# One layer kernel: rows of a tile reordered to (step of chunk, chunk), and the work between the projections laid at fixed steps

## The chip, the cores and the metric

The kernel runs on one core of a Trainium2 chip. The metric is the device time of one execution in microseconds (us); a kernel's time is the median over its runs. The profile records one more execution, with a start and an end for the instructions of each engine: TensorE (PE, with PEld for its weight loads), VectorE (DVE), ScalarE (ACT), GpSimd (POOL) and the queues that issue transfers (SP, and one at ACT).

## What is computed

One layer over 256 rows of width 2048, in float32:

```python
x = x + 0.5 * swiglu(rms_norm(x, ffn1_norm), w_gate, w_up, w_down)       # FFN 1, width 5632
u, q, k, v = split(rms_norm(x, mix_norm) @ w_in)                         # 1024 columns each
y_ssm = S5(u)       # 64 groups of 16 channels, 64 complex states each; z = gelu(y); z * sigmoid(z @ w_glu + b_glu)
y_sb  = sb(rms_norm(q), rms_norm(k), v)                                  # 8 heads of 128
x = x + concat(rms_norm(y_ssm), rms_norm(y_sb)) @ w_out
x = x + 0.5 * swiglu(rms_norm(x, ffn2_norm), ...)                        # FFN 2
x = x + rms_norm((p @ w_ple_proj) * sigmoid(rms_norm(x) @ w_ple_gate))
```

S5 is a diagonal complex recurrence along the rows. The attention has no softmax. With z the scaled score of a query with a key before it, the weight is `exp(log_sigmoid(z) + the sum of log_sigmoid(-z) over the keys between them)`, and 0 for keys that are not before the query.

## The kernel before

**Products.** Each float32 factor is split into two fp32r parts, hi (a cast on ACT, L169) and lo (a subtraction on DVE, L170); a product is hi*hi + lo*hi + hi*lo (L283, L284, L288). `gemm_block` makes 256 rows by 512 columns. It walks the inner dimension in halves of a quarter: a half is 256 inner rows, 12 matmuls of 512 columns. A quarter of the weights (1024 KB) is one transfer on SP into one of three `raw` tiles; its two halves are split into one of four hi and four lo tiles. After each half `step()` is called.

**Steps.** Everything that stands beside the products is attached to steps. `start(g)` puts a generator on a list, and `step()` moves each of them on by one `yield`; `put_off(n, f)` calls `f` at the (n+1)-th step from then. So instructions are written down between the halves. A planner that orders each engine's stream by its own estimates of time may move an instruction ahead of others that it takes to be later; `pin` ties an instruction behind the one written just before it on its engine. The products themselves are not pinned.

**Stages.** FFN 1 also prepares the S5 coefficients (`s5_prep`) and writes them to scratch in DRAM, for four parts q of 16 groups each. Then the layer's middle runs, which the change touches: the projections u (16 halves), q0, k0, q1, k1 (32 halves), v (16 halves), the GLU product of S5 (8 halves of 24 matmuls with 256 columns), and `w_out` (32 halves, the attention side first for each block of columns). After that come FFN 2 and the last embedding.

**S5.** `u_block` takes 512 columns of u out of PSUM; `u_turn` turns them on PE (L678) and brings them on ACT in 32 copies (L686, both halves of u) into an order of (step of chunk, channel) on the partitions. A chunk is 4 rows, so that there are 64 chunks. For each part q, one generator then goes on by a stage per step: the loads from scratch; state matmuls (L705); products with a rotation on DVE (L714 to L717); two sums and two scans over the chunks (L719 to L723); the products back and the shift by one chunk (L728 to L735), where POOL clears the first column (L733); output matmuls (L745 to L749); 16 gelu activations of 32 partitions (L759). POOL writes the decays `dec` (L697) ahead of that. The state matmuls and the output matmuls are four steps apart.

**q and k.** `qk_block` takes a block out on ACT (L773), squares it on DVE (L774), sums (L776), scales each head (L778); at the fourth step after the block PE turns it (L788) and DVE scales it (L792).

**Attention.** Four pairs of heads go through `scores` (with a large negative mask), `logs` (Abs, Exp, Ln on ACT; two DVE instructions on PSUM, L833 and L834) and `weights` (the sums over keys as matmuls into a second PSUM tile, L844 to L851, a subtraction on DVE, L852, and Exp, L853), one stage of one pair per step, all during v. `attn_out` runs during the GLU product. Tiles `aux` in PSUM, two of them, hold everything here that is not a `gemm_block`. `rms` sums the squares (ACT, then POOL, L884) with a matmul (L868).

## Time and profile before

| | |
|---|---|
| runs, median (lowest to highest) | 1942.05 us (1936.94 to 1943.15) |
| the profiled execution | 1942.49 us, of which the span of the profile is 1940.7 us |
| mean granted PE clock in it | 0.991 |
| busy: PE, DVE, ACT, POOL | 1902.7, 1315.6, 1127.0, 36.1 us |
| the layer's middle (u to `w_out`) | from 747.7 to 1111.1 us |

Times in the profile are counted from the start of the span. In a group's row, "x48 | 58.0, 1223 | 42.6 <-ACT" means 48 instructions, 58.0 us busy, 1223 ns for one, and 42.6 us in which the engine was idle just before them, mostly until ACT released them. In a row of the timeline the first two numbers are the start and the duration; a bracket holds the idle time before it and what ended it. Matmuls overlap, so their pitch is read from their starts. A row of windows gives, for each engine, the busy time and the number of instructions, and then the granted PE clock, the DMA share and GB/s.

### The profile page before, as it was taken

The numbers are of one execution on the slowest core, as the hardware profiler recorded it, in microseconds if no ns is written. First come the engines' busy times: TensorE is split into PE (matmuls) and PEld (weight loads), VectorE is DVE, ScalarE is ACT, GpSimd is POOL, SyncE is SP. The second block draws the span as 40 slices with busy tenths as digits, with TensorE's granted clock in tenths as the row PEclk, the third lists the DMA queues.
The fourth block names the chain that finished last, engine by engine and source line by source line (L and its number), as shares of the span: only waits on it lengthen the run. The fifth ranks groups of instructions, "written<-read, shape, count | busy, mean of one in ns | idle before, by whom it ended". The sixth has DMA issues, their size and how long they took to land.

```text
span 1940.7 us, 24021 instructions
## 1 busy us (share of the span) xinstructions
PE 1902.7 (98%) x9148; PEld 1574.8 (81%) x9148; DVE 1315.6 (68%) x1629; ACT 1127.0 (58%) x1294; POOL 36.1 (2%) x52
## 2 busy tenths in 40 slices
PE   9999999999999999988999999999999999999997
PEld 7887788888888888866897888888888888888886
DVE  8995765555688896576666755555555568998855
ACT  7466564444578885746765554444444457887754
POOL 0000000000000000010011000000000000000000
PEclk9999999999999999989999999999999999999999
DMA  9677777666656667554446566666667566666653
GB/s 322 224 229 252 255 239 235 201 212 202 213 191 198 206 206 258 202 203 163 130 159 198 189 194 201 209 215 198 216 195 213 185 222 202 199 205 204 214 189 126
DMA packets 220964, 401.45 MB, mean 207 GB/s; under 512 B 12080, under 2 KB 41904, under 8 KB 220720
## 3 DMA queue, kind: packets, MB, share of 16 engines
q1 hardware_dynamic: 208368, 385.13, 61.1%
q10 hardware_dynamic: 12480, 14.78, 2.1%
q8 instruction: 71, 1.16, 0.2%
q14 instruction: 45, 0.37, 0.1%
HBM read 369.46 MB, written 14.68 MB: 198 GB/s over the span
## 4 chain that ended last, share of the span: by engine, by line
PE 77%; DVE 6%; ACT 4%; issue 2%; DMA 2%; SPq 1%; POOL 1%; DVEq 0%; ACTq 0%; POOLq 0%
PE acc L284 25%; PE acc L283 25%; PE acc L288 24%; DVE wlo L170 2%; DMA raw<-in_ffn_w_down 1%; DVE hlo L170 1%; ACT whi L169 1%; SPq L215 1%; DVE nlo L179 1%; ACT hhi L169 1%; ACT zt L759 1%; DMA dv<-in_ssm_b_laid 0%; DVE cm L544 0%; DMA ceq<-in_ssm_c_laid 0%; DVE mid L202 0%
## 5 line engine op out<-in xcount | busy, mean ns | idle before, releaser
L170 DVE TENSOR_TENSOR wlo<-raw,whi 128x1024 fp32r<-128x1024 f32 x666 | 810.5, 1225 | 460.5 <-ACT whi L169 446.4
L169 ACT CAST whi<-raw 128x1024 fp32r<-128x1024 f32 x666 | 696.6, 1053 | 704.4 <-PE acc L284 647.6
L283 PE MATMUL acc<-whi,nhi 128*128 128x512 f32 x1568 | 618.3, 394 | 4.4 <-ACT whi L169 4.0
L284 PE MATMUL acc<-whi,nlo 128*128 128x512 f32 x1568 | 613.9, 392 | 0.0
L288 PE MATMUL acc<-wlo,nhi 128*128 128x512 f32 x1568 | 421.9, 390 | 0.8 <-DVE wlo L170 0.8
L284 PE MATMUL acc<-whi,hlo 128*128 128x512 f32 x1056 | 411.9, 390 | 0.7 <-DVE hlo L170 0.2
L283 PE MATMUL acc<-whi,hhi 128*128 128x512 f32 x1056 | 411.2, 389 | 0.0
L283 PEld LDWEIGHTS acc<-whi,nhi 128*128 128x128 f32 x1568 | 295.9, 189 | 68.7 <-ACT whi L169 4.9
L288 PEld LDWEIGHTS acc<-wlo,nhi 128*128 128x128 f32 x1568 | 295.0, 188 | 63.7 <-DVE wlo L170 2.0
L284 PEld LDWEIGHTS acc<-whi,nlo 128*128 128x128 f32 x1568 | 296.4, 189 | 60.2
L288 PE MATMUL acc<-wlo,hhi 128*128 128x512 f32 x1056 | 282.3, 389 | 0.0
L284 PEld LDWEIGHTS acc<-whi,hlo 128*128 128x128 f32 x1056 | 198.3, 188 | 44.5 <-DVE hlo L170 3.3
L288 PEld LDWEIGHTS acc<-wlo,hhi 128*128 128x128 f32 x1056 | 198.3, 188 | 41.2
L283 PEld LDWEIGHTS acc<-whi,hhi 128*128 128x128 f32 x1056 | 198.2, 188 | 40.7
L170 DVE TENSOR_TENSOR hlo<-hT,hhi 128x1024 fp32r<-128x1024 f32 x88 | 188.2, 2139 | 49.1 <-ACT hhi L169 49.1
L169 ACT CAST hhi<-hT 128x1024 fp32r<-128x1024 f32 x88 | 192.2, 2185 | 1.7 <-DMA raw<-in_ffn_w_gate 1.7
L202 DVE STREAM_TRANSPOSE mid<-h 128x512 f32<-128x512 f32 x44 | 47.2, 1159 | 0.0
L426 DVE SCALAR_TENSOR_TENSOR h<-acc,sm,sg 128x512 f32<-128x512 f32 x44 | 31.0, 746 | 19.4 <-PE acc L288 19.4
L759 ACT ACTIVATE zt<-aux 32x128 f32<-32x128 f32 x64 | 25.0, 390 | 28.2 <-PE aux L749 27.5
L748 PE MATMUL aux<-rt,cpr 128*64 128x64 f32 x128 | 17.4, 278 | 11.7 <-issue 7.0
L406 ACT ACTIVATE sg<-acc,sm 128x512 f32<-128x512 f32 x44 | 27.7, 682 | 0.4 <-DVE sm L195 0.3
L748 PEld LDWEIGHTS aux<-rt,cpr 128*64 128x64 f32 x128 | 16.4, 191 | 12.4 <-issue 7.5
(233 smaller groups left out, 840.8 us busy)
## 6 DMA issues: line engine op xcount, KB each, us to landing
raw<-in_ffn_w_up SPq DMA_DIRECT2D x88, 1024.0 KB, 5.5
raw<-in_ffn_w_down SPq DMA_DIRECT2D x88, 1024.0 KB, 5.1
raw<-in_ffn_w_gate SPq DMA_DIRECT2D x86, 1024.0 KB, 5.2
raw<-in_w_in SPq DMA_DIRECT2D x32, 1024.0 KB, 5.4
raw<-in_w_out SPq DMA_DIRECT2D x16, 1024.0 KB, 5.2
raw<-in_w_ple_gate SPq DMA_DIRECT2D x16, 1024.0 KB, 5.1
hT<-mid SPq DMA_DIRECT2D x160, 64.0 KB, 4.9
h<-mid SPq DMA_DIRECT2D x128, 32.0 KB, 4.0
```

What stands on the lines that cost most here:

```text
L169: nc.scalar.copy(hi, src)
L170: nc.vector.tensor_tensor(out=lo, in0=src, in1=hi.bitcast(F32), op=ALU.subtract)
L179: nc.vector.scalar_tensor_tensor(out=lo[:, j, :], in0=src[:, j, :], scalar=scale, in1=hi[:, j, :].bitcast(F32), op0=ALU.mult, op1=ALU.subt ...
L202: nc.vector.transpose(mid[:, :, t, :, k0 : k0 + nk].rearrange("p q b f -> p f q b"), src.rearrange("p (f q b) -> p f q b", f=nk, q=4),)
L215: nc.sync.dma_start(out[32 * q : 32 * q + 32, :, 32 * i : 32 * i + 32, :], mid[32 * i : 32 * i + 32, q])
L283: nc.tensor.matmul(ps[t], lhsT=lh, rhs=hi[:, j, :], start=start and j == 0, stop=False)
L284: nc.tensor.matmul(ps[t], lhsT=ll, rhs=hi[:, j, :], start=False, stop=False)
L288: nc.tensor.matmul(ps[t], lhsT=lh, rhs=lo[:, j, :], start=False, stop=stop and j == 1)
L406: nc.scalar.activation(sg[:, t * NB : (t + 1) * NB], pg[t], AF.Silu, scale=xn.rs(t))
L426: nc.vector.scalar_tensor_tensor(out=hh[:, t * NB : (t + 1) * NB], in0=pu[t], scalar=xn.rs(t), in1=sg[:, t * NB : (t + 1) * NB], op0=ALU.m ...
L748: nc.tensor.matmul(o, lhsT=ld["cpr"][:, cs], rhs=pr[:, rs], start=False, stop=False)
L759: nc.scalar.activation(zv[32 * r : 32 * r + 32, 2 * (q % 2) : 2 * (q % 2) + 2, :, t], yv[32 * t : 32 * t + 32, :, r, :], AF.Gelu_apprx_tanh,)
```

## The change

The host hands x, its turned copy and p to the kernel with the rows of each tile of 128 in the order (step of chunk, chunk), so that partition 32*s + c holds row 4*c + s, and puts the output's rows back. The masks of the attention follow that order: a small input `not_ahead` is loaded through SP in place of two POOL instructions. With this order:

- `u_turn` is two DVE transposes in blocks of 32 by 32. The 16 PE transposes and the 32 ACT copies go.
- S5's stages are put off to fixed steps: part q has its state matmuls at step 12 + 8q, counted from the first half of u, then its DVE stages at +3, +4 and +5, its output matmuls at +7 and gelu at +9. DVE handles real and imaginary parts in one instruction; the first column is cleared on DVE; the decays and the loads for part q have steps of their own, and `rot` has two tiles. Gelu is one activation of 128 partitions, followed by 16 transfers of 32 KB per pair of parts that bring the channels to the partitions.
- q/k: squares and scaling move to ACT, the turn is at the fifth step, and the scaling follows two steps later.
- Attention: each stage of a pair has its own step. The sums over keys are accumulated into the scores' own PSUM tile with masks of -1, so that L834, L852 and the second tile go. Pairs 0 and 1 begin at steps 5 and 6 of v, pairs 2 and 3 at steps 17 and 19, which are steps 1 and 3 of the GLU product. `attn_out` comes at step 16 and at step 28 (the fourth half of `w_out`).
- v is taken out of PSUM on ACT. `w_out` begins with the S5 side of the first two blocks of columns; the sum for S5's norm is one step later.
- Most matmuls of S5 and of the attention are pinned.

```diff
-        for to, op, scale in ((tri_r, ALU.is_gt, 1.0), (late_r, ALU.is_ge, -(2.0 ** 100))):
-            u = com("h")[:, :P]
-            nc.gpsimd.affine_select(
-                out=u, in_=ones, compare_op=op, fill=0.0, base=0, pattern=[[-1, P]], channel_multiplier=1
-            )
-            nc.scalar.activation(to, u, AF.Copy, scale=scale)
+
+        u = com("h")[:, :P]
+        nc.sync.dma_start(u, a["not_ahead"])
+        nc.scalar.activation(tri_r, u, AF.Copy, scale=-1.0)
+        nc.scalar.activation(late_r, u, AF.Copy, scale=-(2.0 ** 100))
         nc.scalar.copy(ident_r, ident)
-        nc.scalar.copy(ones_r, ones)
+        nc.scalar.activation(all_r, ones, AF.Copy, scale=-1.0)
...
-        put_off(2, u_turn, pool, n, us)
+        put_off(1, u_turn, pool, n, us)
 
     def u_turn(pool, n, us):
-        pt = aux()
+        ua[n] = get(pool, f"ua{n}")
         for t in range(TT):
-            for b in range(4):
-                pin(nc.tensor.transpose(
-                    pt[:, b * T + t * P : b * T + (t + 1) * P], us[:, t * NB + b * P : t * NB + (b + 1) * P], ident
-                ))
-        ua[n] = get(pool, f"ua{n}")
-        pv = pt.rearrange("p (b c s) -> p b c s", b=4, s=SL)
-        uv = ua[n].rearrange("p (b q c) -> p b q c", b=4, q=4)
-        for q in range(4):
-            for s in range(SL):
-                nc.scalar.copy(uv[32 * s : 32 * s + 32, :, q, :], pv[32 * q : 32 * q + 32, :, :, s])
+            nc.vector.transpose(
+                ua[n].rearrange("p (r t c) -> p r t c", t=TT, c=32)[:, :, t, :],
+                us[:, t * NB : (t + 1) * NB].rearrange("p (r h) -> p r h", h=32),
+            )
 
     def s5_main(pool, zpool):
...
+        def load(q, names):
+            for n in names:
+                ld[q][n] = get(pool, n, bufs=2 if n == "rot" else 1)
+                nc.sync.dma_start(ld[q][n], scr[n][q])
+
+        def decays(q):
+            ld[q]["dec"] = get(pool, "dec")
+            dvw = ld[q]["dec"].rearrange("p (i r c) -> p i r c", i=2, c=NC)
+            for i in range(2):
+                nc.gpsimd.tensor_copy(
+                    dvw[:, i], rho4[:, 8 * q : 8 * q + 8].unsqueeze(2).to_broadcast([P, 8, NC])
+                )
+            nc.gpsimd.memset(dvw[:, :, :, 0:1], 0.0)
...
+        def both(w):
+            return w.rearrange("p (i c) -> p i c", i=2)
+
+        def turns(q, i):
+            return ld[q]["rot"][:, i * 512 : (i + 1) * 512].unsqueeze(1).to_broadcast([P, 2, 512])
+
+        def forth(q):
+
+            u, ps = st[q]
+            ta, tb = (get(pool, "rt", bufs=3) for _ in range(2))
+            tt(out=both(ta), in0=both(ps), in1=turns(q, 0), op=ALU.mult)
+            tt(out=both(tb), in0=both(ps), in1=turns(q, 1), op=ALU.mult)
+            st[q] = u, ta, tb
+
+        def scan(q):
+            u, ta, tb = st[q]
+            tt(out=ta[:, :512], in0=ta[:, :512], in1=tb[:, 512:], op=ALU.add)
+            tt(out=ta[:, 512:], in0=ta[:, 512:], in1=tb[:, :512], op=ALU.subtract)
+            g = get(pool, "rt", bufs=3)
+            nc.vector.tensor_tensor_scan(
+                out=g, data0=ld[q]["dec"], data1=ta, initial=0.0, op0=ALU.mult, op1=ALU.add
+            )
+            st[q] = u, g
+
+        def back(q):
+            u, g = st[q]
             tc_, td, pr = (get(pool, "rt", bufs=3) for _ in range(3))
-            tt(out=tc_[:, :512], in0=g[:, :512], in1=rr, op=ALU.mult)
-            tt(out=td[:, :512], in0=g[:, 512:], in1=ri, op=ALU.mult)
-            tt(out=tc_[:, 512:], in0=g[:, 512:], in1=rr, op=ALU.mult)
-            tt(out=td[:, 512:], in0=g[:, :512], in1=ri, op=ALU.mult)
+            tt(out=both(tc_), in0=both(g), in1=turns(q, 0), op=ALU.mult)
+            tt(out=both(td), in0=both(g), in1=turns(q, 1), op=ALU.mult)
...
-            nc.gpsimd.memset(v[2][:, :, :, 0:1], 0.0)
+            nc.vector.memset(v[2][:, :, :, 0:1], 0.0)
...
-                zt[q // 2] = get(zpool, f"zt{q // 2}")
-            zv = zt[q // 2].rearrange("p (b c t) -> p b c t", b=4, t=SL)
-            yv = yp[:, :512].rearrange("p (b r c) -> p b r c", b=2, r=4)
-            for r in range(4):
-                for t in range(SL):
-                    nc.scalar.activation(
-                        zv[32 * r : 32 * r + 32, 2 * (q % 2) : 2 * (q % 2) + 2, :, t],
-                        yv[32 * t : 32 * t + 32, :, r, :], AF.Gelu_apprx_tanh,
-                    )
-            yield
+                zs[n] = com("mid")[:, :1024]
+            nc.scalar.activation(
+                zs[n][:, (q % 2) * 512 : (q % 2) * 512 + 512], st[q][:, :512], AF.Gelu_apprx_tanh
+            )
+            if q % 2:
+                zt[n] = get(zpool, f"zt{n}")
+                start(channels(n))
+
+        def channels(n):
+
+            zv = zt[n].rearrange("p (b s c) -> p b s c", b=4, s=SL)
+            sv = zs[n].rearrange("p (b r c) -> p b r c", b=4, r=4)
+            for s in range(SL):
+                for r in range(4):
+                    nc.sync.dma_start(zv[32 * r : 32 * r + 32, :, s, :], sv[32 * s : 32 * s + 32, :, r, :])
+                yield
+
+        load(0, ("m1r", "m1i", "rot", "cpr", "cpi", "m3"))
+        decays(0)
+        for q in range(NQ):
+            a0 = 11 + 8 * q
+            if q:
+                put_off(a0 - 4, load, q, ("m1r", "m1i", "rot"))
+                put_off(a0 + 4, load, q, ("cpr", "cpi", "m3"))
+                put_off(a0 - 3, decays, q)
+            for steps, stage in ((0, states), (3, forth), (4, scan), (5, back), (7, outputs), (9, gelu)):
+                put_off(a0 + steps, stage, q)
...
-        nc.vector.tensor_tensor(out=sq, in0=qs, in1=qs, op=ALU.mult)
+        nc.scalar.activation(sq, qs, AF.Square)
...
-        put_off(3, qk_turn, pool, dst, n, qs, gain, scale)
-
...
-        dst[n] = get(pool, f"{gain}{n}")
-        nc.vector.tensor_scalar(dst[n], pt, col(gain, 0), scale, op0=ALU.mult, op1=ALU.mult)
-
-    def attn_scores(pool):
-
-        tt = nc.vector.tensor_tensor
+        put_off(1, qk_scale, pool, dst, n, pt, scale)
+
+    def qk_scale(pool, dst, n, pt, scale):
+        dst[n] = get(pool, f"{'q' if dst is qT else 'k'}{n}")
+        nc.scalar.activation(dst[n], pt, AF.Copy, scale=scale)
...
-            sp, w = get(pool, "sp", W, 2), get(pool, f"w{hp}", W)
-            nc.scalar.activation(sp, ps[:, :W], AF.Abs)
-            nc.scalar.activation(sp, sp, AF.Exp, scale=-1.0)
-            st[hp] = ps, sp, w
+                ))
+            st[hp] = ps
+
+        def exps(hp):
+            ps, sp = st[hp], get(pool, "sp", W, 2)
+            pin(nc.scalar.activation(sp, ps[:, :W], AF.Abs))
+            pin(nc.scalar.activation(sp, sp, AF.Exp, scale=-1.0))
+            st[hp] = ps, sp
 
         def logs(hp):
 
-            ps, sp, w = st[hp]
-            nc.scalar.activation(sp, sp, AF.Ln, bias=1.0)
+            ps, sp = st[hp]
+            pin(nc.scalar.activation(sp, sp, AF.Ln, bias=1.0))
             nc.vector.scalar_tensor_tensor(out=sp, in0=ps[:, :W], scalar=0.0, in1=sp, op0=ALU.max, op1=ALU.add)
-            tt(out=w, in0=ps[:, :W], in1=sp, op=ALU.subtract)
+
+        def parts(hp):
+            ps, sp = st[hp]
             hi = pool.tile([P, W], F32R, tag="sph", name=uid("sph"), bufs=2)
             lo = pool.tile([P, W], F32R, tag="spl", name=uid("spl"), bufs=2)
             split(hi, lo, sp)
-            st[hp] = w, (hi, lo)
+            st[hp] = ps, (hi, lo)
+
+        def passes(hp):
+
+            ps, both = st[hp]
+            for u in both:
+                pin(nc.tensor.matmul(
+                    ps[:, :NB], lhsT=tri_r, rhs=u[:, :NB], start=False, stop=False, skip_group_check=True
+                ))
+                pin(nc.tensor.matmul(
+                    ps[:, :NB].rearrange("p (j t) -> p j t", j=2)[:, :, P:], lhsT=all_r, rhs=u[:, NB:W],
+                    start=False, stop=True, skip_group_check=True,
+                ))
+                pin(nc.tensor.matmul(
+                    ps[:, NB:W], lhsT=tri_r, rhs=u[:, NB:W], start=False, stop=True, skip_group_check=True
+                ))
 
         def weights(hp):
...
-            tt(out=w, in0=w, in1=cp[:, :W], op=ALU.subtract)
-            nc.scalar.activation(w, w, AF.Exp)
-            sbp[hp] = w
-
-        for stage, pair in ((scores, 0), (logs, 0), (weights, 0), (scores, 1), (logs, 1), (weights, 1)):
-            for hp in (2 * pair, 2 * pair + 1):
-                stage(hp)
-                yield
+            sbp[hp] = get(pool, f"w{hp}", W)
+            nc.scalar.activation(sbp[hp], st[hp][0][:, :W], AF.Exp)
+
+        for hp, b in enumerate(begins):
+            for steps, stage in ((0, scores), (2, exps), (4, logs), (5, parts), (7, passes), (9, weights)):
+                put_off(b + steps, stage, hp)
...
+        def evacuate():
...
+        put_off(1, evacuate)
+
+    def glu_in(zs, k):
+        hi, lo = halves("h")
+        split(hi, lo, zt[k].rearrange("p (j t) -> p j t", j=4), pinned=True)
+        zs.append((hi, lo))
...
-            nc.vector.tensor_tensor(out=y, in0=sg, in1=zt[n], op=ALU.mult)
+            for t in range(TT):
+
+                su, zu = (u.rearrange("p (c s t k) -> p c s t k", c=4, s=SL, t=TT)[:, :, :, t, :] for u in (sg, zt[n]))
+                yu = y.rearrange("p (c t s k) -> p c s t k", c=4, s=SL, t=TT)[:, :, :, t, :]
+                nc.vector.tensor_tensor(out=yu, in0=su, in1=zu, op=ALU.mult)
...
-        return parts, rms(2, sq_acc, SW)
+        return parts, rms(3, sq_acc, SW)
...
+    s5_main(pool, mixp)
     for n in range(2):
         u_block(pool, n, gemm_block(nm, w_in, n * NB, KD), nm)
-    s5 = start(s5_main(pool, mixp))
+    q_scale = small(1)
+    nc.vector.tensor_scalar(q_scale, col("q_norm", 0), DH ** -0.5, None, op0=ALU.mult)
     for n in range(2):
-        qk_block(mixp, qT, n, gemm_block(nm, w_in, q0 + n * NB, KD), nm, "q_norm", DH ** -0.5)
-        qk_block(mixp, kT, n, gemm_block(nm, w_in, k0 + n * NB, KD), nm, "k_norm", 1.0)
-    finish(s5)
+        qk_block(mixp, qT, n, gemm_block(nm, w_in, q0 + n * NB, KD), nm, q_scale)
+        qk_block(mixp, kT, n, gemm_block(nm, w_in, k0 + n * NB, KD), nm, col("k_norm", 0))
     s5p.close()
     pool = atp.enter_context(phase("attn"))
-    zs = glu_in()
-    sb = []
-    sc = start(attn_scores(pool))
+    zs, ysb = [], []
+    sqa = get(pool, "sqa", T)
+    put_off(5, glu_in, zs, 0)
+    put_off(7, glu_in, zs, 1)
+    attn_scores(pool, (4, 5, 16, 18))
+    put_off(15, attn_out, pool, 0, ysb, sqa)
     vt = [get(pool, f"v{t}") for t in range(TT)]
     for n in range(2):
         ps = gemm_block(nm, w_in, v0 + n * NB, KD)
         for t in range(TT):
-            nc.vector.tensor_scalar(vt[t][:, n * NB : (n + 1) * NB], ps[t], nm.rs(t), None, op0=ALU.mult)
-    finish(sc)
-    attn = start(attn_out(pool, sb))
+            nc.scalar.activation(vt[t][:, n * NB : (n + 1) * NB], ps[t], AF.Copy, scale=nm.rs(t))
+    put_off(11, attn_out, pool, 1, ysb, sqa)
     yss, rss = glu(pool, zs)
-    finish(attn)
-    ysb, rsb = sb
+    rsb = rms(8, sqa, NH * DH)
     w_out = a["w_out"][0]
-    for n in range(ND):
-        for y, r, w in ((ysb, rsb, w_out[SW:, :]), (yss, rss, w_out[:SW, :])):
-            ps = gemm_block(lambda k: y[k], w, n * NB, SW // P)
-            for t in range(TT):
-                nc.vector.scalar_tensor_tensor(
-                    out=xt[t][n], in0=ps[t], scalar=r[0][:, t : t + 1], in1=xt[t][n], op0=ALU.mult, op1=ALU.add
-                )
-        put_off(2, n2.block, n)
+    for n, side in ((0, 0), (1, 0), (0, 1), (1, 1), (2, 0), (2, 1), (3, 0), (3, 1)):
+        y, r = ((yss, rss), (ysb, rsb))[side]
+        ps = gemm_block(lambda k: y[k], w_out[side * SW : (side + 1) * SW, :], n * NB, SW // P)
+        for t in range(TT):
+            nc.vector.scalar_tensor_tensor(
+                out=xt[t][n], in0=ps[t], scalar=r[0][:, t : t + 1], in1=xt[t][n], op0=ALU.mult, op1=ALU.add
+            )
+        if side:
+            put_off(2, n2.block, n)
...
+def steps_order(n):
+    return np.arange(n).reshape(-1, P // SL, SL).transpose(0, 2, 1).reshape(-1)
+
...
+    order = steps_order(a["x"].shape[1])
+    x = a["x"][0][order]
+    step = order[:P]
```

157 lines of the change are left out of this document (59 added, 98 removed).

## The prediction, made before the result was known

> **What bounds the kernel now.** I read the page first.
>
> ```profile
> PE 1902.7 (98%) x9148; PEld 1574.8 (81%) x9148; DVE 1315.6 (68%) x1629; ACT 1127.0 (58%) x1294; POOL 36.1 (2%) x52
> ```
>
> PE is busy for 98% of the span, so a gain must be time in which PE waits or runs slowly, or work of PE that goes. The windows show where that time is. The five rows are u, q/k, v, GLU and `w_out`, cut where their first product starts.
>
> ```profile
> 747.70:793.00 45.30, 45.30 (x209) 37.71 (x208) 23.36 (x30) 27.78 (x45) 0.00 (x0) 1.00 0.66 220
> 793.00:933.00 140.00, 123.18 (x1058) 102.32 (x1056) 94.03 (x120) 78.66 (x132) 9.66 (x10) 0.93 0.57 193
> 933.00:989.70 56.70, 54.87 (x266) 46.01 (x265) 40.32 (x45) 44.62 (x49) 0.00 (x0) 1.00 0.41 135
> 989.70:1017.90 28.20, 28.20 (x226) 27.78 (x225) 17.29 (x23) 18.46 (x36) 6.78 (x8) 1.00 0.44 152
> 1017.90:1111.10 93.20, 90.75 (x402) 74.90 (x401) 63.82 (x82) 51.14 (x73) 6.22 (x7) 0.98 0.62 200
> ```
>
> PE is idle for 140.0 - 123.18 = 16.8 us in q/k, where its clock is also granted at 0.93 only; 1.8 us in v; 2.45 us in `w_out`. Next, the timeline of PE gives what the work of q/k costs when nothing waits.
>
> ```profile
> 773.07 0.39 PE L283 MATMUL acc<-whi,nhi 128*128 128x512 f32 x1
> 775.79 0.39 PE L283 MATMUL acc<-whi,nhi 128*128 128x512 f32 x1
> 795.83 1.15 PE L705 MATMUL aux<-ua,m1r 128*64 128x64 f32 x32
> 797.85 0.50 PE L283 MATMUL acc<-whi,nhi 128*128 128x512 f32 x1
> 809.84 0.33 PE L745 MATMUL aux<-ua,m 128*64 128x64 f32 x2
> 812.96 0.50 PE L283 MATMUL acc<-whi,nhi 128*128 128x512 f32 x1
> 867.50 0.37 PE L748 MATMUL aux<-rt,cpr 128*64 128x64 f32 x1 [4.70 <-POOL rt L733]
> 872.92 0.56 PE L283 MATMUL acc<-whi,nhi 128*128 128x512 f32 x1
> ```
>
> A half takes 775.79 - 773.07 = 2.72 us, a part's state matmuls 797.85 - 795.83 = 2.02, its output matmuls 812.96 - 809.84 = 3.12. After the 4.70 us stall nearly the same output matmuls took 872.92 - 867.50 = 5.42: a stall also costs some 2.3 us of slow clock behind it. The work of q/k is 32 halves (87.0), four times both kinds (8.1 and 12.5) and four turns at about 0.8 (3.2): 110.8. The stage took 140.0, so **29.2 us** are lost: 16.8 idle, about 9.8 to the clock (140 x 0.07), the rest in the changes between kinds of matmul. Who ends those waits, in u and q/k:
>
> ```profile
> PE aux L748 <- issue: 7.0, 2, 4.0
> PE aux L748 <- POOL rt L733: 4.7, 1, 4.7
> PE aux L788 <- DVE sg L778: 3.8, 1, 3.8
> PE aux L705 <- ACT zt L759: 1.3, 1, 1.3
> ```
>
> That is all 16.8. The output matmuls (L748) take 11.7 of it; they need what DVE makes from the state matmuls.
>
> ```profile
> L170 DVE TENSOR_TENSOR wlo<-raw,whi 128x1024 fp32r<-128x1024 f32 x48 | 58.0, 1223 | 42.6 <-ACT whi L169 40.4 <-PE acc L288 2.1
> L723 DVE TENSOR_TENSOR_SCAN rt<-dec,rt 128x512 f32<-128x512 f32 x8 | 9.5, 1214 | 0.0
> L720 DVE TENSOR_TENSOR rt<-rt,rt 128x512 f32<-128x512 f32 x4 | 2.8, 688 | 0.0
> L778 DVE TENSOR_TENSOR sg<-sg,sm 128x1024 f32<-128x1024 f32 x3 | 3.7, 1228 | 0.1
> L776 DVE TENSOR_REDUCE sm<-h 128x8 f32<-128x1024 f32 x3 | 3.6, 1211 | 0.0
> L792 DVE TENSOR_SCALAR q_norm<-aux,gains 128x1024 f32<-128x1024 f32 x2 | 2.6, 1284 | 4.7 <-PE aux L788 4.7
> 859.87 7.32 POOL L697 COPY dec<-rho 128x512 f32<-128x512 f32 x1 [25.31 <-DVE rt L723]
> ```
>
> A part has 12 DVE instructions of about 512 columns (0.69 each) and two scans (1.21): 10.7 us. The four halves between its state and its output matmuls are 10.9 us of PE, in which DVE also owes four weight splits (4 x 1.22 = 4.9). It needs 15.6 and has 10.9: 4.7 too little, as large as the waits of 4.0 and 4.7. One of these is charged to POOL, whose clearing of a column stood behind a `dec` copy of 7.32 us.
>
> **The change, part by part.**
>
> *S5's stages.* From the end of the state matmuls to the output matmuls there are now seven halves, 19.0 us. DVE's part: four instructions of 1024 columns (nearest row L170, 1.22), four of about 512, scans as before (2.4), a small clear: 10.2. It owes seven splits (8.6) too, and one q/k block: a sum and a scaling (1.21 + 1.23) and small ones, about 3.5. That makes 22.3 against 19.0, but up to four lo tiles (4.9) can be ahead, so it just fits. Over a whole period of eight halves, PE needs 21.8 + 2.0 + 3.1 + 0.8 = 27.7 and DVE 10.2 + 9.8 + 3.5 = 23.5, 85%. So DVE is not the bound, though lumps may be late. The clear on DVE ends the 4.70 behind POOL; `dec` itself is started seven halves before its scan, and two copies at the worst 7.32 fit 19.0. If DVE's lead is gone, the stage waits again (first rival). Between a residue of 0 and all 29.2 I take one wait of the smallest kind the stage shows, 1.3, for each of four parts: 5.2. **-24.0 us.**
>
> *The turn of u.* The PE transposes go:
>
> ```profile
> L678 PE MATMUL aux<-ident,sg 128*128 128x128 f32 x16 | 2.1, 272 | 0.0
> L202 DVE STREAM_TRANSPOSE mid<-h 128x512 f32<-128x512 f32 x44 | 47.2, 1159 | 0.0
> L686 ACT COPY ua<-aux 32x256 f32<-32x256 f32 x32 | 11.7, 364 | 1.8 <-PE aux L678 1.5
> L759 ACT ACTIVATE zt<-aux 32x128 f32<-32x128 f32 x64 | 25.0, 390 | 28.2 <-PE aux L749 27.5
> ```
>
> At 0.8 per block, **-1.6 us** (2.1 at most). Two DVE transposes per block (2.3 us) lie in u, where DVE is busy for 23.4 of 45.3; the state matmuls come two steps later. Without that cover a block would cost PE up to 2.3. The 11.7 us of copies and 25.0 us of gelu on ACT are hidden now (its waits are for PE), but for the 1.3 of L705, which I have put in the residue. The gelu's new transfers, 32 KB each, end by step 49 and are read at step 54, four halves of cover.
>
> *q/k on ACT.* A square and a scaling move from DVE (L792, 1.28) to ACT, which has 78.7 busy of 140.0 and loses most of the 36.7: nothing. The turn (L788) has one half more, which covers most of its 3.8.
>
> *v.* The 1.8 idle is a first sum over keys that waited for DVE's split. It now comes two steps behind that split, and DVE loses L834 and L852: **-1.8** (0 if a scoring tile is still late; pair 1 needs the tile that the last k turn leaves, with a half between).
>
> *GLU.* Pairs 2 and 3 move here from v. The matmuls are the same; ACT is what fills up:
>
> ```profile
> L895 PE MATMUL aux<-w,v 128*128 128x256 f32 x16 | 4.8, 379 | 0.0
> L169 ACT CAST whi<-raw 128x1024 fp32r<-128x1024 f32 x57 | 59.3, 1049 | 49.3 <-PE acc L284 42.5 <-PE acc L945 5.2 <-DMA h<-mid 1.7
> L832 ACT ACT_TABLE_LOAD x4 | 5.1, 1283 | 0.1
> L177 ACT ACTIVATE nhi<-h,gains 128x256 fp32r<-128x256 f32 x8 | 3.4, 499 | 0.7 <-DVE h L962 0.7
> L832 ACT ACTIVATE sp<-sp 128x768 f32<-128x768 f32 x4 | 3.4, 845 | 0.0
> L958 ACT ACTIVATE sg<-acc,gains 128x256 f32<-128x256 f32 x8 | 3.1, 478 | 0.0
> L883 ACT ACTIVATE sqp<-h 128x256 f32<-128x256 f32 x7 | 2.7, 407 | 0.5 <-POOL sqg L884 0.5
> ```
>
> From step 17 to step 28, where the last attention product needs pair 3's weights, ACT has 12 casts (12.6), ten instructions of 768 columns (Abs, Exp, Ln, split and final Exp, twice: 8.5), 8 sigmoids (3.8), 12 scalings (6.0), 12 squares (4.9) and, by the order Ln, Exp, Ln, Sigmoid, Exp after a first Sigmoid, 6 table loads (7.7): 43.5. PE has 8 GLU halves (28.2 less the 4.8 of the attention products, 23.4), 4 halves (10.9) and the scores and sums of two pairs, 32 matmuls of the same sizes as the attention products' 32, so an estimated 4.8 again: 39.1. ACT is 4.4 over, and the four hi tiles that it can have ahead are worth 4.2. I take **+3**, between 0 and 4.4 with a slow clock of 2.3 twice (9.0).
>
> [...]
>
> *`w_out`.* Its 2.45 us wait:
>
> ```profile
> 1017.87 0.40 PE L283 MATMUL acc<-whi,nhi 128*128 128x512 f32 x1
> 1029.15 0.71 PE L868 MATMUL aux<-ones,sqg 128*128 128x128 f32 x4 [2.45 <-POOL sqg L884]
> 1023.81 2.15 DVE L179 SCALAR_TENSOR_TENSOR nlo<-h,gains,nhi 128x256 fp32r<-128x256 f32 x4
> ```
>
> The sum over squares comes a half (2.72) later, so this goes. But the S5 side now comes first, and its second part is needed two halves (5.4) after the GLU product; before it was done 1023.81 + 2.15 - 1017.87 = 8.1 after. That leaves a wait of 2.7 in its place: **0**.
>
> *The masks.* One small load for two POOL instructions, in FFN 1's first blocks, hidden behind the products: 0. Uncovered it would hold SP for as long as its tile is in use; the longest such wait quoted below is 10.2, and the weights are 16.3 ahead.
>
> Sum: -24.0 - 1.6 - 1.8 + 3 + 0 = -24.4, against the profiled execution's own 1942.5 (span 1940.7 and 1.8 around it): **1918 us**. The median of the runs, 1942.05, is 0.4 lower.
>
> **The rivals.**
>
> *S5's stages still wait for DVE.* If the planner lets no split run ahead, 22.3 against 19.0 leaves 3.3 per part and 2.3 of slow clock: 22.4 for four instead of 5.2. Then 1918 + 17 = 1935. For it speaks that DVE has lumps of 10 us; against it, that it has 15% of slack.
>
> *ACT bounds the GLU stage.* The full 9.0 instead of 3, and the sums over keys of pair 3 late once more (2.3): 1926. For it: 43.5 against 39.1; against it, that casts can be ahead and squares can be late. [...]
>
> *Slower: S5's loads stand before the weights on SP.* At steps 24 and 32 six loads of 512 KB come at once, at step 40 three, and those of one tile wait for the part before. Weights that stand behind them are late.
>
> ```profile
> SPq L694 <- DVE rt L731: 28.4, 3, 10.2
> ```
>
> SP has already stood up to 10.2 us in front of a load. With no lead left, three such places cost 3 x (10.2 + 2.3) = 37.5: 1918 + 37.5 = 1956. It decides from the point where the wait is longer than the lead of the weights, three raw tiles or six halves, 16.3 us. Against it: in the rows of waits above nothing of PE's is late by a weight transfer.
>
> *It doesn't do what it says.* If the planner moves the products around the pinned matmuls so that the waits stay, only the turns go: 1941.
>
> **How the numbers follow.** Chances: forecast 0.56, ACT 0.13, DVE 0.15, as before 0.07, slower 0.09. A measurement of this kernel can tell about 0.3% (5.8 us) from no change, so faster means below 1936.2: the forecast, ACT, and most of DVE (0.13): 0.82. Same: 0.07 + 0.02 = 0.09. Slower: 0.09. The range reaches from all losses gone (29.2 + 1.6 + 1.8 and, in `w_out`, 2.45 and its clock, 93.2 x 0.02 = 1.9: 37.0, so 1905) up past the DVE rival to 1938; the two cases above it hold 0.16.
>
> **What would show it.** In q/k: PE's idle time below 6 us and the clock above 0.97; L748 (its new line) out of PE's waits; a stage of about 113 us (110.8 + 5.2, less a turn and the first state matmuls, which move into u). No PE transposes in u. In the GLU windows: ACT nearly full, and a short wait of the attention products or the sums for ACT. A PE wait for a `whi` that waited for a transfer in q/k would show the SP rival. I am wrong if q/k keeps more than half of its 29 us, or if GLU and `w_out` take back more than 10.

## The result, and the profile after

The changed kernel takes 1905.36 us (median of 4 runs, 1904.67 to 1911.35), beside 1940.05 us (1936.94 to 1943.15) of the kernel before on the same chip: a ratio of 0.9828, 95% interval 0.9801 to 0.9855. Forecast were 1918 and a range from 1905 to 1938, so the time lies 0.4 us above the lower end of the range. The profiled execution took 1904.67 us, its span is 1902.9 us, its mean granted clock 0.998.

The page of after, busy times and the chain that ended last:

```profile
PE 1887.9 (99%) x9132; PEld 1564.6 (82%) x9132; DVE 1301.0 (68%) x1600; ACT 1106.5 (58%) x1216; POOL 34.0 (2%) x50
PE 84%; DVE 4%; DMA 2%; issue 2%; ACT 1%; SPq 1%; DVEq 0%; ACTq 0%
```

DVE and ACT have hardly less work than before (1315.6 and 1127.0). What went is time in which PE stood or ran slowly. The windows of after, cut as before at the first product of u, q/k, v, GLU and `w_out`:

```profile
744.47:791.10 46.63, 46.63 (x265) 38.73 (x264) 31.94 (x39) 22.18 (x29) 3.20 (x3) 1.00 0.72 246
791.10:901.10 110.00, 110.00 (x985) 92.04 (x984) 80.98 (x93) 56.46 (x61) 6.55 (x6) 1.00 0.70 228
901.10:953.10 52.00, 52.00 (x250) 43.78 (x248) 29.94 (x31) 39.56 (x44) 0.00 (x0) 1.00 0.55 191
953.10:979.30 26.20, 26.20 (x216) 25.99 (x215) 14.22 (x19) 24.22 (x38) 3.53 (x5) 1.00 0.36 121
979.30:1072.70 93.40, 93.40 (x430) 77.90 (x429) 67.75 (x90) 56.71 (x85) 9.61 (x10) 1.00 0.58 193
```

In all five rows PE's busy time is the length of the window and the clock is 1.00: from 744.47 to 1072.7 PE never waits. The middle is 328.2 us long and was 363.4 (747.70 to 1111.10): 35.2 less, of which q/k has 30. The order of PE in a part, by its timeline (the first rows of a part's state matmuls, of the half behind them, of its output matmuls and of the next half):

```profile
832.85 1.15 PE L712 MATMUL aux<-ua,m1r 128*64 128x64 f32 x32
...
834.87 0.50 PE L284 MATMUL acc<-whi,nhi 128*128 128x512 f32 x1
...
855.03 0.33 PE L764 MATMUL aux<-ua,m 128*64 128x64 f32 x2
...
858.14 0.50 PE L284 MATMUL acc<-whi,nhi 128*128 128x512 f32 x1
```

The state matmuls take 2.02 us and the output matmuls 3.11, what they took before where nothing waited; between them lie seven halves and a turn. What is left of PE's waits in the whole kernel lies outside the middle (the longest; a row gives the sum, how many there are, and the longest of them):

```profile
PE acc L289 <- DVE wlo L171: 1.8, 1, 1.8
...
```

### The profile page after: what moved, and what is told of

It is laid out like the page before. It is cut to its first block, busy times and chain, and to the rows that moved or that the text cites. A ratio compares the mean times of both kernels' runs of the same rounds, so it can differ in the third digit from the quotient of the medians.

```text
span 1902.9 us, 23907 instructions
## 1 busy us (share of the span) xinstructions
PE 1887.9 (99%) x9132; PEld 1564.6 (82%) x9132; DVE 1301.0 (68%) x1600; ACT 1106.5 (58%) x1216; POOL 34.0 (2%) x50
## 3 DMA queue, kind: packets, MB, share of 16 engines
q8 instruction: 71, 1.16, 0.3%
## 4 chain that ended last, share of the span: by engine, by line
PE 84%; DVE 4%; DMA 2%; issue 2%; ACT 1%; SPq 1%; DVEq 0%; ACTq 0%
PE acc L284 27%; PE acc L285 27%; PE acc L289 27%; DMA raw<-in_ffn_w_down 1%; DVE wlo L171 1%; DVE hlo L171 1%; ACT hhi L168 1%; SPq L216 1%; DVE nlo L180 1%; DMA ceq<-in_ssm_c_laid 1%; PE aux L712 0%; PE acc L991 0%; PE acc L986 0%; PE acc L982 0%; PE aux L631 0%
## 5 line engine op out<-in xcount | busy, mean ns | idle before, releaser
L203 DVE STREAM_TRANSPOSE mid<-h 128x512 f32<-128x512 f32 x44 | 47.0, 1154 | 0.0
L178 ACT ACTIVATE nhi<-h,gains 128x256 fp32r<-128x256 f32 x40 | 23.8, 657 | 0.2 <-DVE h L1007 0.2
L701 POOL COPY dec<-rho 128x512 f32<-128x512 f32 x8 | 10.5, 1346 | 732.2 <-DVE rt L738 565.1
L180 DVE SCALAR_TENSOR_TENSOR nlo<-h,gains,nhi 128x256 fp32r<-128x256 f32 x40 | 23.0, 628 | 0.6 <-ACT nhi L178 0.6
```

Of the source, the lines that this page charges most:

```text
L178: nc.scalar.activation(hi[:, j, :], src[:, j, :], AF.Copy, scale=scale)
L180: nc.vector.scalar_tensor_tensor(out=lo[:, j, :], in0=src[:, j, :], scalar=scale, in1=hi[:, j, :].bitcast(F32), op0=ALU.mult, op1=ALU.subt ...
L203: nc.vector.transpose(mid[:, :, t, :, k0 : k0 + nk].rearrange("p q b f -> p f q b"), src.rearrange("p (f q b) -> p f q b", f=nk, q=4),)
L701: nc.gpsimd.tensor_copy(dvw[:, i], rho4[:, 8 * q : 8 * q + 8].unsqueeze(2).to_broadcast([P, 8, NC]))
```

## The experiments

The question is which part of the new order ended the waits before the output matmuls: the distance of seven steps (A in the quoted texts, where they use letters), the pins (C), gelu in one ACT instruction (D), squares and scaling of q and k on ACT (E), or that a part comes every eight steps and not every six. A second question is why GLU and `w_out` did not take back what the forecast gave them.

The start of u in the profiles moved between 741.9 and 748.2 us, among kernels with the same FFN 1 too. So beside the time I give the length of the middle, from the first product of u to the first of FFN 2, in each kernel's one profiled execution:

| kernel | median, us | ratio to before, 95% interval | middle, us |
|---|---|---|---|
| before | 1940.05 | | 363.4 |
| after | 1905.36 | 0.9828 (0.9801 to 0.9855) | 328.2 |
| gap4 | 1907.34 | 0.9834 (0.9817 to 0.9851) | 334.0 |
| nopins | 1902.15 | 0.9806 (0.9791 to 0.9821) | 328.2 |
| old_gap6 | 1924.14 | 0.9912 (0.9891 to 0.9933) | 349.0 |
| old_gap6_pins | 1927.13 | 0.9932 (0.9910 to 0.9954) | 350.8 |
| gap4_gelu64 | 1909.27 | 0.9850 (0.9829 to 0.9872) | 332.5 |
| gap4_qkdve | 1908.81 | 0.9850 (0.9822 to 0.9879) | 334.7 |
| gap4_both | 1909.16 | 0.9854 (0.9829 to 0.9879) | 336.5 |
| gap7_both | 1902.77 | 0.9823 (0.9794 to 0.9851) | 328.2 |
| gap4_period6 | 1910.03 | 0.9841 (0.9823 to 0.9859) | 334.3 |
| gap4_phase4 | 1911.49 | 0.9844 (0.9827 to 0.9861) | 335.2 |
| old_period8 | 1920.49 | 0.9896 (0.9880 to 0.9912) | 347.6 |
| act_more | 1910.40 | 0.9841 (0.9823 to 0.9859) | 334.1 |

Each ratio is to the kernel before as it was measured beside that experiment: 1940.81 for the first four experiments, 1936.89 for the next four, 1940.85 for the last four.

**gap4: the old distance in the new kernel.**

```diff
-                put_off(a0 + 4, load, q, ("cpr", "cpi", "m3"))
-                put_off(a0 - 3, decays, q)
-            for steps, stage in ((0, states), (3, forth), (4, scan), (5, back), (7, outputs), (9, gelu)):
+                put_off(a0 + 1, load, q, ("cpr", "cpi", "m3"))
+                put_off(a0 - 5, decays, q)
+            for steps, stage in ((0, states), (1, forth), (2, scan), (3, back), (4, outputs), (6, gelu)):
```

> The changed kernel with one size put back: S5's output matmuls four steps behind the state matmuls instead of seven (stages at +1, +2, +3, +4, gelu at +6; the second loads at +1 and the decays three steps earlier, so that neither is late). Pins, row order and ACT's work stay as changed. Theory A (the distance between the stages is what ended the waits): DVE needs 10.2 + 4 x 1.22 = 15.1 us in 10.9, so PE waits before each part's output matmuls for some 2 to 5 us and runs slowly for 2 behind it; the q/k stage is 15 to 25 us longer than the changed kernel's 110.0, the time 1920 to 1930. Theory B (what ended them is that the matmuls are pinned, or that ACT and DVE have less work): within 3 us of the changed kernel, 1905.

Its waits of PE in the middle:

```profile
PE aux L765 <- DVE rt L751: 3.0, 3, 1.1
PE aux L766 <- DVE rt L751: 0.3, 1, 0.3
```

The waits come back, but small: 3.3 us where the kernel before had 11.7, the middle 5.7 longer than after's. By the time alone gap4 can't be told from after (the intervals overlap). So four steps are too few by about 1 us a part, not by the 4.7 of the prediction, and most of the loss had another cause. The time is where theory B put it, but the next experiments take B's two reasons away as well.

**nopins: after without the new pins.** The pins go from the matmuls of S5 and attention, from the activations Abs, Exp and Ln and from the casts of the GLU product's input, as here for one (`free` hands back the instruction and does nothing else):

```diff
-                    pin(nc.tensor.matmul(o, lhsT=ld[q]["cpr"][:, cs], rhs=pr[:, rs], start=False, stop=False))
+                    free(nc.tensor.matmul(o, lhsT=ld[q]["cpr"][:, cs], rhs=pr[:, rs], start=False, stop=False))
```

> The changed kernel with all steps as changed, but the state, output, scoring and attention matmuls, and the Abs, Exp, Ln and GLU casts on ACT, not pinned, so that the planner may move them ahead by its own estimates (as before, only the turns, the first sum over keys and the sums of squares are pinned). Theory A (the distance alone is enough): within 3 us of the changed kernel. Theory C (the waits of before came from matmuls that the planner put too early in PE's stream): the output matmuls float back to some four halves behind the state matmuls, and 10 to 25 us of waits return, 1915 to 1930.

The middle is 328.2 us long, as in after, without a wait of PE. The pins carry nothing here.

**old_gap6 and old_gap6_pins: more distance in the kernel before.** Two empty steps are put between the state and the output matmuls, so that the outputs are six steps behind and a part comes every eight steps; the second kernel also pins S5's matmuls.

```diff
+            yield
             yield
             rr, ri = ld["rot"][:, :512], ld["rot"][:, 512:]
...
+            yield
             yield
             tc_, td, pr = (get(pool, "rt", bufs=3) for _ in range(3))
```

And in old_gap6_pins, as here for one:

```diff
-                    nc.tensor.matmul(o, lhsT=ld["cpr"][:, cs], rhs=pr[:, rs], start=False, stop=False)
+                    pin(nc.tensor.matmul(o, lhsT=ld["cpr"][:, cs], rhs=pr[:, rs], start=False, stop=False))
```

> The kernel before with two empty steps put in for each part of S5, so that its output matmuls are written six halves behind the state matmuls instead of four; nothing pinned, row order, gelu and copies as before. Theory A: in 16.3 us DVE has 10.7 for S5, 7.3 for splits and up to 6 for a q/k block, with splits ahead; the 11.7 us of waits at the output matmuls fall to 0 to 5, and with the slow clock the time falls by 10 to 20, 1920 to 1930. Theory C: the planner moves the unpinned matmuls to where it takes them to be ready, so the waits stay and the time is 1935 to 1942.

> The same two empty steps in the kernel before, and the state and output matmuls of S5 pinned behind the half they are written after. Theories A and C both expect the waits at the output matmuls to go, but for POOL's clearing behind a copy of the decays (up to 4.7): 1918 to 1926. If the relief of ACT and DVE is what counts, the waits stay: 1935 to 1942.

Waits of PE in the middle of old_gap6:

```profile
PE aux L790 <- DVE sg L780: 8.8, 3, 2.9
...
```

The output matmuls are out of the list. The turns of q and k (L790 is L788 of before) have taken 8.8 us in their place, where they had 3.8: in this order DVE scales a block too late for the fourth step. The pins change nothing that can be measured (old_gap6_pins came out 1.1 us above its expected range). Both kernels also have a part every eight steps. The kernel old_period8 below has that alone, with a middle of 347.6 beside 349.0 here, so the added distance brings nothing beyond the longer period.

**gap4_gelu64, gap4_qkdve, gap4_both, gap7_both: the reliefs of ACT and DVE undone.** At four steps, either gelu goes back to 16 small activations per part, or squares and scaling go back to DVE, or both; and both at seven steps.

```diff
-            nc.scalar.activation(
-                zs[n][:, (q % 2) * 512 : (q % 2) * 512 + 512], st[q][:, :512], AF.Gelu_apprx_tanh
-            )
+            for r in range(4):
+                for s in range(SL):
+                    nc.scalar.activation(
+                        zv[32 * r : 32 * r + 32, 2 * (q % 2) : 2 * (q % 2) + 2, s, :],
+                        yv[32 * s : 32 * s + 32, :, r, :], AF.Gelu_apprx_tanh,
+                    )
...
-        nc.scalar.activation(sq, qs, AF.Square)
+        nc.vector.tensor_tensor(out=sq, in0=qs, in1=qs, op=ALU.mult)
...
-        nc.scalar.activation(dst[n], pt, AF.Copy, scale=scale)
+        nc.vector.tensor_scalar(dst[n], pt, scale, None, op0=ALU.mult)
```

> The kernel with S5's output matmuls four steps behind (as in the run before it of that name), and gelu again as 16 activations of 32 partitions per part on ACT, written straight to the channels' partitions, without the transfers. At four steps alone PE waited 3.3 us in all and the time was 1907. Theory D (before, ACT's 6.4 us of small gelus held up the casts of the weights, DVE's splits bunched and S5 began late): each part's chain begins some 2 to 3 us later and PE waits 2 to 4 us for each of three parts, with slow clock behind: 1914 to 1924. Theory E (what counted was the DVE work of q and k): no change, 1907 within 3.

> Four steps, and q/k's square and scaling back on DVE (1.2 and 1.3 us per block), gelu as one activation. Theory E: 2.5 us more of DVE per block come into the parts' windows, PE waits 2 to 4 us per part: 1914 to 1924. Theory D: no change, 1907 within 3.

> Four steps with both: small gelus on ACT, and q/k's square and scaling on DVE. If the relief of ACT and DVE together is what let four steps do, the waits of the kernel before return here, 3 to 5 us per part: 1920 to 1932. If neither counts (the steps' phase against the q/k blocks does it), 1907 within 4.

> The changed kernel with seven steps and both reliefs taken back: small gelus on ACT, q/k's square and scaling on DVE. Theory A in its weaker form (seven steps are enough whatever ACT and DVE do, as six steps were in the kernel before): no waits before the output matmuls, at most the turns of q and k wait up to 3 us each; 1905 to 1914. If the relief is needed at seven steps too: 1915 to 1930.

At four steps the three kernels keep to 1909 us, with waits like gap4's; gap4_both has the most, four of 4.0 us together, the longest of 1.6.

gap7_both has no wait of PE in the middle, which is 328.2 us long. With a part every eight steps neither relief is needed, and seven steps alone end the last waits.

**old_period8: the kernel before with a part every eight steps, nothing else.** Two empty steps stand behind gelu; the distance of four stays.

```diff
                         yv[32 * t : 32 * t + 32, :, r, :], AF.Gelu_apprx_tanh,
                     )
             yield
+            yield
+            yield
```

> The kernel before with two empty steps after gelu, so that a part comes every eight steps in place of six, and the four steps between its state and output matmuls stay. Rate theory: the 11.7 us before the output matmuls mostly go, and what is left is what the kernel with the outputs six steps behind kept (1924): 1922 to 1930. Distance theory (four steps are too few for the old order of DVE's instructions): the waits stay, 1933 to 1941.

Its waits of PE in the middle:

```profile
PE aux L790 <- DVE sg L780: 3.6, 3, 1.7
PE aux L748 <- POOL rt L733: 2.6, 2, 1.3
...
PE aux L749 <- DVE rt L735: 0.2, 1, 0.2
```

Two empty steps per part, with no work removed and no distance added, take the waits before the output matmuls from 11.7 to 2.8 us, and the middle from 363.4 to 347.6: 15.8 of the 35.2 us by which the whole change shortens it. (The times give 20.4 of 34.7, but they also hold what FFN 1 differs by; u begins 3.8 us earlier in this profile than before.) DVE ends only 0.2 of those 2.8. It also ends the 3.6 at the turns of q and k, but these stand one half ahead of the output matmuls, so that PE's wait there gives DVE time for what comes next. The other 2.6 are POOL's, whose timeline has the clear (L733) behind the same kind of long copy as before:

```profile
831.00 6.18 POOL L697 COPY dec<-rho 128x512 f32<-128x512 f32 x1 [27.83 <-DVE rt L723]
...
837.31 0.12 POOL L733 MEMSET rt<- 128x16 f32 x1
862.74 6.18 POOL L697 COPY dec<-rho 128x512 f32<-128x512 f32 x1 [25.31 <-DVE rt L723]
...
869.05 0.12 POOL L733 MEMSET rt<- 128x16 f32 x1
```

The clears end at 837.43 and 869.17; two of the waiting output matmuls start at 837.49 and 869.23, each after 1.28. The change takes the clear to DVE.

**gap4_period6 and gap4_phase4: the old rate, and another phase, in the new kernel.**

```diff
-            a0 = 11 + 8 * q
+            a0 = 11 + 6 * q
```

> The kernel after with four steps between the state and the output matmuls (as gap4, 1907.3) and, in place of eight, six steps from part to part: states at 12 + 6q. Rate theory (in the kernel before a part came every six halves, in which DVE owes about as much as PE: 10.2 + 6 x 1.22 + its share of q/k, some 22 against PE's 22, so DVE falls behind whatever the distance): the waits before the output matmuls return, 2 to 4 us at two or more parts, with a slow clock behind each, 1915 to 1928. Distance or phase theory: nothing returns, 1905 to 1910.

```diff
-            a0 = 11 + 8 * q
+            a0 = 15 + 8 * q
```

> As gap4 (four steps of distance, eight from part to part), but all of S5 four steps later: states at 16 + 8q, so that the DVE stages of a part fall on the halves in which DVE also sums, scales and copies a block of q or k. Phase theory (what made DVE late before was that its lumps of S5 and of q/k fell together): waits of 2 to 4 us before the output matmuls or the q/k turns at each part, 1914 to 1924. Rate theory: the work per period is the same, 1905 to 1911. The last part's outputs come four steps later too, in v; that alone is no cost by either.

Waits of PE in the middle, gap4_period6 first:

```profile
PE aux L765 <- DVE rt L751: 3.1, 3, 1.0
```

```profile
PE aux L765 <- DVE rt L751: 3.7, 4, 1.3
```

Neither brings the old waits back, though the rate theory expected them at six steps: the middle is 0.4 and 1.2 us longer than gap4's, which one profile of each can hardly tell. So six steps are not too few by themselves, and the phase against the blocks of q and k isn't the cause in the new order. The windows from the first state matmul to the last output matmul tell the kernels apart; before, old_period8, gap4_period6, after:

```profile
795.83:902.10 106.27, 93.25 (x931) 78.05 (x930) 76.66 (x100) 57.74 (x99) 9.66 (x10) 0.92 0.58 200
```

```profile
792.06:902.03 109.97, 103.53 (x1009) 86.05 (x1008) 86.49 (x115) 67.26 (x110) 14.04 (x10) 1.00 0.64 220
```

```profile
777.86:867.19 89.33, 86.11 (x915) 70.35 (x914) 71.14 (x76) 38.33 (x42) 9.76 (x9) 1.00 0.68 229
```

```profile
778.09:886.41 108.32, 108.32 (x1029) 90.90 (x1028) 88.14 (x98) 53.95 (x58) 9.75 (x9) 1.00 0.73 245
```

PE's own work in these windows is 22, 28, 22 and 31 halves of 2.72, four times 2.02 and 3.12, and three, four, one and two turns of 0.8: 82.8, 99.9, 81.2 and 106.5 us. DVE's busy time over it is 0.93, 0.87, 0.88 and 0.83; the window is longer than the work by 23.5, 10.1, 8.1 and 1.8 us. DVE's busy time in gap4_period6 is less than before over as many halves because q/k's squares and scaling are gone and only a part of the second block of q or k falls in the window. The loss is largest where DVE's work came nearest to PE's. That fits a rate but does not show one: old_period8 shows that the period counts in the kernel before, and not by which engine. ACT is a rival that no run rules out. With a part every six steps the 16 small gelus of one part end only about when the state matmuls of the next begin (820.28 and 818.66 for part 1); in old_period8 they end 3.9 us ahead of them (816.44 and 820.33). Six steps with the small gelus, or with both reliefs undone, were not tried.

**act_more: does ACT stand at its limit around the GLU product?** Pairs 2 and 3 get three copies more, which nothing reads:

```diff
             pin(nc.scalar.activation(sp, sp, AF.Exp, scale=-1.0))
+            for _ in range(3 if hp > 1 else 0):
+                pin(nc.scalar.activation(get(pool, "more", W), sp, AF.Copy))
```

> The kernel after with three more ACT copies of 128x768 behind the Exp of attention pairs 2 and 3, which nobody reads: about 5 us of ACT work more in the stretch around the GLU product, 36.6 + 5.0 = 41.6 against its 39.0 us. If ACT stood at its limit there, as the prediction had it with +3: PE waits of 2 to 5 us and a slow clock behind them, 1908 to 1912. If the casts that ACT has ahead (four hi tiles, 4.2 us) and the squares that can be late cover it: 1902 to 1906, no new wait.

The groups of ACT from 952.57 to 997.36, the waits of PE in the middle, and the window from the end of after's GLU product to the start of pair 3's attention product here:

```profile
L871 ACT ACTIVATE more<-sp 128x768 f32<-128x768 f32 x6 | 5.1, 848 | 0.1
L1001 ACT ACT_TABLE_LOAD x2 | 2.6, 1283 | 0.0
```

```profile
PE acc L284 <- ACT whi L168: 3.4, 2, 2.1
```

```profile
979.30:997.40 18.10, 14.67 (x59) 11.18 (x58) 12.26 (x14) 17.88 (x27) 5.34 (x5) 0.91 0.33 112
```

The 5.1 us of copies, with a second table load for the sigmoids (1.28) that the later order brings, make 3.4 us of waits, a clock of 0.91 behind them, and a middle that is 5.8 us longer. So after has next to no slack on ACT there, though it waits for nothing. (The times of the two kernels alone, with intervals that overlap, would not tell this; the waits and the middle do.)

## Why the prediction came out as it did

The mechanism held in the main: the waits went, PE's clock came back, and nothing new stands in their place. The size was too small: the sum was -24.4 and the middle shows -35.2. The time fell inside the range by 0.4 us, where the runs of this kernel differ by 6.7; that it fell inside is luck. Compared stage by stage, with what moved between stages set aside (scores and sums over keys 1.47 and 0.93 per pair, the attention products 2.5 per two pairs, as both timelines show them):

| term | forecast | measured |
|---|---|---|
| S5's stages and the turn of u (u and q/k together) | -25.6 | 185.3 to 156.6: -28.7 |
| v | -1.8 | -2.4 |
| GLU | +3 | 0 |
| `w_out` | 0 | -4.3 |
| sum | -24.4 | -35.4 |

(The 0.2 beside the middle's 35.2 comes from the sizes set aside, which differ a little between the two kernels.)

*S5's stages: right, and its residue too large.* The residue of 5.2 for waits did not come. What is left of the losses is in the changes between kinds of matmul, 1.8 us in the last of the four windows above. The rows of DVE from u to the last turn of q and k:

```profile
L738 DVE TENSOR_TENSOR_SCAN rt<-dec,rt 128x1024 f32<-128x1024 f32 x4 | 9.1, 2283 | 0.0
L747 DVE TENSOR_TENSOR rt<-rt,rot 128x1024 f32<-128x1024 f32 x4 | 6.1, 1524 | 0.0
L729 DVE TENSOR_TENSOR rt<-aux,rot 128x1024 f32<-128x1024 f32 x4 | 4.9, 1224 | 2.5 <-PE aux L712 2.5
L679 DVE STREAM_TRANSPOSE ua<-sg 128x512 f32<-128x512 f32 x4 | 2.6, 683 | 0.0
```

The scan at 2.28 (2.4 forecast) and the instructions of 1024 columns at 1.22 to 1.52 (1.22) bear out the cost of a part. DVE's share of a period, 85% in the forecast, is 0.81 in the window of after (88.14 of 108.32).

*The diagnosis behind it: wrong in its size, and in part in its cause.* The step "it needs 15.6 and has 10.9: 4.7 too little" charged four halves with all four splits. It allowed four lo tiles to be ahead where it looked at seven halves, and not where it looked at four. By that account any kernel with four steps would lose 4.7 a part; gap4 loses 1.1 at most in one wait for DVE, and old_period8 0.2. It also took ACT's small gelus for hidden. The timelines of ACT, DVE and PE before show what they did to part 1, whose state matmuls end at 820.68 (they start at 818.66 and take 2.02):

```profile
813.84 6.44 ACT L759 ACTIVATE zt<-aux 32x128 f32<-32x128 f32 x16
820.31 2.00 ACT L169 CAST whi<-raw 128x1024 fp32r<-128x1024 f32 x2
```

```profile
821.39 2.36 DVE L170 TENSOR_TENSOR wlo<-raw,whi 128x1024 fp32r<-128x1024 f32 x2 [7.42 <-ACT whi L169]
823.67 0.68 DVE L714 TENSOR_TENSOR rt<-aux,rot 128x512 f32<-128x512 f32 x1
```

```profile
836.22 0.45 PE L748 MATMUL aux<-rt,cpr 128*64 128x64 f32 x2 [2.98 <-issue]
```

The casts stand behind the gelus. DVE is idle for 7.42 us until the first of them, then has two splits at once, and begins the part 3.0 us after its state matmuls; the output matmuls wait for 2.98. (The profile names no releaser there; DVE's first L735 ends 0.1 us earlier.) Part 3 begins 5.0 us late and waits for 4.03. Part 0, with no gelu ahead of it, begins 0.1 us late and doesn't wait. So DVE was late after standing idle, and not only for its four splits. Whether this order or its share of 0.93 of PE's work counts for more, no run separates.

The wait of 4.70 behind POOL, which the prediction took for another sight of the same lateness, is for the most part a cause by itself: DVE had ended its last instruction for that part at 864.45, 3 us before the wait ended, and such waits stay in small in old_period8. The sum did not suffer from the wrong diagnosis, because it takes the 29.2 us from the rows and only argues that they go.

*GLU: +3 was 0, by two mis-sizings.* ACT's 43.5 were built as mean times count. The window of after from the first GLU product to pair 3's attention product shows 36.62 of 38.96:

```profile
953.10:992.06 38.96, 38.96 (x275) 36.69 (x274) 24.29 (x30) 36.62 (x59) 8.62 (x10) 1.00 0.39 136
```

In the groups of ACT in it the cause can be read:

```profile
L178 ACT ACTIVATE nhi<-h,gains 128x256 fp32r<-128x256 f32 x8 | 3.4, 508 | 0.2 <-DVE h L1007 0.2
L999 ACT ACTIVATE sg<-acc,gains 128x256 f32<-128x256 f32 x8 | 3.1, 479 | 0.0
```

Eight times 508 is 4.06, and the group was busy for 3.4: neighbours overlap, by about 0.1 us each. The rows that the prediction quoted showed it (8 x 499 beside 3.4). And there are five table loads and not six: both last Exps (984.27 and 989.32) came behind the second group of sigmoids (981.38), so that none stands between the two groups. PE's 39.1 were right (38.96). That ACT fills up was right too, as act_more shows.

The load between the second sigmoids and pair 2's last Exp took its own 1.28 us, as forecast, and next to nothing beside it: in the timeline of after's ACT it begins 0.02 us behind the sigmoids, and Exp 0.02 us behind it:

```profile
981.38 1.57 ACT L999 ACTIVATE sg<-acc,gains 128x256 f32<-128x256 f32 x4
982.97 1.28 ACT L902 ACT_TABLE_LOAD   x1
984.27 0.81 ACT L902 ACTIVATE w<-aux 128x768 f32<-128x768 f32 x1
```

*`w_out`: the wait that took the place did not come.* The S5 side's second part was ready 8.2 us after the GLU product (8.1 forecast; the row of DVE, with PE's half behind it):

```profile
985.79 1.68 DVE L180 SCALAR_TENSOR_TENSOR nlo<-h,gains,nhi 128x256 fp32r<-128x256 f32 x4 [0.58 <-ACT nhi L178]
...
986.61 0.40 PE L284 MATMUL acc<-whi,nhi 128*128 128x512 f32 x1
```

The forecast put its need two halves after the product. It forgot two things: both sums over keys of pairs 2 and 3 (0.93 each) now stand among these halves, which puts the third half at 986.61, 7.3 after 979.28; and that half begins with the first of the four tiles, ready at about 986.2 (985.79 + 1.68/4). So the 2.45 of POOL and its slow clock (93.2 x 0.02 = 1.9) went without a return: 4.3. The margin is half a microsecond.

*v, the masks, q/k on ACT:* as forecast, within 0.6. That the squares' move is worth nothing is borne out by gap7_both, though only at eight steps to a part.

*The rivals.* DVE is not late; ACT is full but doesn't bind; the planner did not move the products so that the waits stay. S5's loads do stand on SP, and its queue's waits in after show for how long (the longest of them):

```profile
SPq L695 <- PE aux L766: 15.4, 3, 7.9
```

7.9 us is half of the lead of 16.3 that the weights have, so nothing of PE's is late by it. FFN 1, which the forecast left alone, is 3.2 shorter in this profile; nopins and gap7_both, with the same FFN 1 as after, differ from it by 2.6 and 2.3, so I make nothing of that.

## What to carry to other kernels

Before counting one chain against its gap, compare each engine's work with TensorE's over one period of the schedule, and see what stands in front of the chain on the other engines. Here two empty steps in each period, with no work removed, brought 15.8 of the 35.2 us. When the output matmuls no longer waited, the q/k turns did (8.8 us in old_gap6), so move a stage together with all that wait for the same engine. Take an engine's load from the busy time of a group, not from mean times count, where neighbours overlap.
